# Modulation weights in tiles of 2048 columns, four blocks of 512 to the array together

## The chip, the cores and the metric

The kernel runs on one core of a Trainium2 chip. The metric is the device time of one execution in microseconds (us), and the time of a version is the median of its runs. TensorE (PE) does the matrix products, VectorE (DVE), ScalarE (ACT) and GpSimd (POOL) the elementwise work. SyncE's queue (SP) issues nearly all transfers between the device's memory and the on-chip memory, in order: an issue that waits holds up those behind it. A product's result lies in PSUM, a small accumulation memory of banks of 512 columns by 128 partitions. All data is f32.

## The reference, cut to what matters

The model has two layers on 1024 latent tokens and 256 context tokens of width 1024. Each layer begins with a modulation: two vectors (`c` for the latents, `c_ctx` for the context) pass through silu and are multiplied by a matrix of 1024 x 6144; the six slices of the result shift, scale and gate what follows.

```
s_lat = silu(c); s_ctx = silu(c_ctx)
for layer in range(2):
    sh1, sc1, g1, sh2, sc2, g2 = split(s_lat @ ada_w[layer] + ada_b[layer], 6)
    csh1, ..., cg2             = split(s_ctx @ ada_w[layer] + ada_b[layer], 6)
    h = modulate(rmsnorm(x, norm_mix_w[layer]), sh1, sc1)      # the context likewise
    x = x + g1 * mixer(h)                                      # layer 0: attention + SSD, layer 1: mLSTM
    x = x + g2 * mlp(modulate(rmsnorm(x, ...), sh2, sc2))
out = rmsnorm(x, final_norm_w)
```

Each mixer begins with an input projection, a product of `h` with a matrix of some 2100 or 3100 columns, parts of which go through a convolution of five taps along the tokens.

## The kernel before, in words

**The modulation.** Its weight, 2 x 24 MB, is far larger than the two vectors that it multiplies, so the vectors are the stationary operand and the weight streams through the array. `ada_group` (L182) computes a group, 2048 of the 6144 columns of one layer (three groups to a layer). It walks the 1024 input rows in eight steps `k` of 128. In a step the 2048 columns are four blocks of 512. The stationary operand has only 32 columns, so each block uses a strip of 32 columns of the array and writes its own 32 partitions of one PSUM bank: block g goes to partitions 32g to 32g+31. The argument `per` is the number of blocks that one weight tile holds. With `per=4` a step is one load of 128 x 2048 (1 MB) and four products; with `per=2` it is two loads of 128 x 1024 (512 KB), each with two products. In the trace each product appears as two instructions, so a tile of two blocks is a row of `x4` and one of four blocks is `x8`. After a step the generator yields. After the eighth, DVE copies the bank (`ada_rows`), PE turns it with eight small instructions (`ada_t`), and DVE adds the bias into `mods`. The bank is the only one of its kind (`bufs=1`), so a group begins when the one before has been turned.

**Where the groups run.** The first group (layer 0, group 0) is computed in `start` (L433) with `per=4` and eight buffers, beside the load of `x`. Three more (`(0,1)`, `(0,2)`, `(1,0)`) run as a filler inside `in_proj0` (L487), the other two (`(1,1)`, `(1,2)`) as a filler inside `in_proj1` (L1283), all with `per=2`, from a pool of two and of three buffers. The method `fill(n)` advances the filler by n steps, and is called each time a block of a projection has been evacuated.

**The projections.** `lin` (L383) multiplies a weight tile of 128 columns with the three token blocks (512, 512 and 256 tokens). Weight and data are each split into a high and a low part, and three products (`mm3`, L99 to L101) make one f32 product: 24 instructions for a block. In `in_proj0` eight such weight tiles feed the convolution (`conv_silu`, L401, five DVE operations of 1284 elements). Then come four tiles for the low-rank inputs of the attention (`lc`, `lsq`, `lhi`, `llo`: pool `s0a`) and four for the gate `z`. When the convolution is through, the filler is replaced by `back_states` (L731), the backward chain of the state-space scan, from the pool `bwd`. `in_proj1` has eight tiles for its convolution and then the values.

**Pools.** Pools are laid out as a stack in the on-chip memory. A pool opened where a closed one was waits, tile by tile, for the last reader of the old tile. `ada1` stands below the pool of the convolution and stays open to the end of `in_proj0`; `ada2` stands below `s1`, `raw1` and `kN`.

**The order of the work.** The order of instructions on each engine is fixed when the kernel is built: a planner takes them by priority (the order of the program, or further ahead where `high_priority` says so; `ahead`, L84, gives each filler step in `in_proj1` a lead of 400) and by its own estimate of when their operands are ready. On the chip each engine then runs its list in order. The four lines that step the modulation:

```
nc.sync.dma_start(out=raw, in_=w[k * 128:(k + 1) * 128, c0:c0 + per * 512])
for g in range(per):
    nc.tensor.matmul(out=ps[32 * (n + g):32 * (n + g) + 32, :], lhsT=self.s32[:, 2 * k:2 * k + 32],
                     rhs=raw[:, g * 512:(g + 1) * 512], start=k == 0, stop=k == KT - 1)
```

Of the kernel before, what the change touches and what calls it, by code (L numbers as in the profile page):

```python
# [67 lines left out]
class Kernel:  # L68
# [418 lines left out]
    def in_proj0(self):  # L487
# [23 lines left out]
        wp, pp = self.wp0, self.pp0  # L511
        with ExitStack() as es:
# [1 line left out]
            xp = self.pool("xnbn", side="right", stack=es)  # L514
            xn = xp.tile([128, NC, 512], F32, name="xn")
            bn = xp.tile([128, NC, 256], F32, name="bn")
            ap = self.pool("ada1", bufs=2, stack=es)
            stp = self.pool("ps_l0", bufs=2, space=PSUM, stack=es)
            self.filler = self.ada_fill(ap, stp, ((0, 1), (0, 2), (1, 0)), 2)


            with ExitStack() as es2:
# [27 lines left out]
            with ExitStack() as es2:  # L550
# [14 lines left out]
                for m in range(8):  # L565
# [17 lines left out]
                    if m < 6:  # L583
                        last = (m, co)
            self.fill(99)
            nc.sync.dma_start(out=self.xnd, in_=xn)
            nc.sync.dma_start(out=self.bnd, in_=bn)
            bp = self.pool("bwd", bufs=2, stack=es)
# [694 lines left out]
    def in_proj1(self):  # L1283
        nc, I = self.nc, self.ins
        w_in = I["od_w_in"][0]
        dram = self.dram.tile
        self.od = dram([128, 8, SEQ], F32, name="od")
        self.vd = dram([128, NC, D], F32, name="vd")
        self.kTd = dram([128, 4, NT], F32, name="kTd")
        self.qTd = dram([128, 4, SEQ], F32, name="qTd")  # L1290
        self.kNd = dram([128, NC, 512], F32, name="kNd")
        self.o1 = ExitStack()
        op = self.pool("out1", side="right", stack=self.o1)
        self.uN, self.wt, self.em = (op.tile([128, 160], F32, name=n) for n in ("uN", "wt", "em"))
        self.keepc = op.tile([128, 2, NC, 4], F32, name="keepc")
        gb = op.tile([128, 32], F32, name="gbias")
        for i, n in enumerate(("od_i_bias", "od_f_bias")):
            nc.sync.dma_start(out=gb[:, 16 * i:16 * i + 16],
                              in_=I[n].rearrange("e d h -> (e d h)").unsqueeze(0).to_broadcast([128, 16]))
        every, lat = [(b, ALL_BLOCKS[b]) for b in (0, 2, 1)], list(enumerate(LAT_BLOCKS))  # L1300
        self.in1, self.banks = ExitStack(), ExitStack()
        p1 = self.pool("ps_m1", space=PSUM, stack=self.in1)
        p2 = self.pool("ps_m2", space=PSUM, stack=self.banks)
        self.pp = pp = Banks(m1=(p1, "m1", 2), m2=(p2, "m2", 3), st=(p2, "st", 2), ada=(p2, "ada", 1), mm=(p2, "m2", 3),
                             a=(p2, "m2", 3))
        self.wp1 = wp = self.pool("w1", bufs=2, stack=self.in1)
        vps = ExitStack()
        vp = self.pool("wv1", bufs=2, side="right", stack=vps)
        with ExitStack() as es2:
            ap = self.pool("ada2", bufs=3, stack=es2)  # L1310
            self.filler = self.ahead(self.ada_fill(ap, pp, ((1, 1), (1, 2)), 2), 400)
            sp = self.pool("s1", bufs=2, stack=es2)
            with self.tc.high_priority(400):
                raws = self.conv_raw(self.pool("raw1", stack=es2), 2)
            kNp = self.pool("kN", bufs=2, stack=es2)

            def by_token(m, co):
                kN = kNp.tile([128, NC, 128], F32, name="kN")
                for c0 in range(0, NC, 4):
                    n = min(4, NC - c0)  # L1320
                    o = c0 * 128 + (4 if c0 >= 8 else 0)
                    ps = pp.tile([128, 512], F32, name="kN_ps", tag="a")
                    for i in range(n):
                        self.turn(ps[:, i * 128:(i + 1) * 128], co[:, o + i * 128:o + (i + 1) * 128])
                    nc.scalar.copy(out=kN[:, c0:c0 + n, :], in_=ps[:, :n * 128].rearrange("p (c f) -> p c f", f=128))
                nc.sync.dma_start(out=self.kNd[:, :, m * 128:(m + 1) * 128], in_=kN)

            last = None
            self.fill(4)
            for m in (4, 5, 6, 7, 0, 1, 2, 3):  # L1330
                whi, wlo = self.w4 if m == 4 else self.load_w(wp, w_in[:, m * 128:(m + 1) * 128])
                r = raws[m % 2]

                def evac(b, t0, nb, ps):
                    o = t0 + 2 if t0 < SEQ else t0 + 6
                    with self.tc.high_priority(400 if m == 4 else 0):
                        nc.scalar.copy(out=r[:, o:o + nb], in_=ps[:, :nb])
                    self.fill(2 if b == 0 else 1)

                self.lin(pp, whi, wlo, 128, self.h, every if m >= 4 else lat, evac, tag="m1")  # L1340
                if last is not None:
                    by_token(*last)
                    last = None
                co = self.conv_silu(sp, r, m, 1, None, m >= 4)
                if m >= 4:
                    last = (m - 4, co)
                    nc.sync.dma_start(out=self.kTd[:, m - 4, 0:SEQ], in_=co[:, 0:SEQ])
                    nc.sync.dma_start(out=self.kTd[:, m - 4, SEQ:NT], in_=co[:, SEQ + 4:NT + 4])
                else:
                    nc.sync.dma_start(out=self.qTd[:, m, :], in_=co[:, 0:SEQ])  # L1350
            self.fill(99)


        with ExitStack() as es2:
            tp = self.pool("ml_g", stack=es2)
            self.gN = tp.tile([128, NC, 32], F32, name="gN")
            for j in range(4):
                n = 256 if j else 288
                hi = vp.tile([128, KT, 288], F32R, name="wv_hi")
                lo = vp.tile([128, KT, 288], F32R, name="wv_lo")  # L1360
                for i in range(2 if j else 3):
                    raw = wp.tile([128, KT, 128], F32, name="w_raw", tag="w_raw")
                    c0, M = (1024 + j * 256 + i * 128, 128) if i < 2 else (3072, 32)
                    nc.sync.dma_start(out=raw[:, :, :M], in_=w_in[:, c0:c0 + M].rearrange("(k p) f -> p k f", p=128))
                    self.split_w(raw[:, :, :M], hi[:, :, i * 128:i * 128 + M], lo[:, :, i * 128:i * 128 + M])
                for c in range(NC):
                    b = min(c // 4, 2)
                    o = c * 128 - ALL_BLOCKS[b][0]
                    ps = pp.tile([128, 512], F32, name="v1_ps", tag="m1")
                    for k in range(KT):  # L1370
                        xh, xl = (self.h[b][i][:, k, o:o + 128] for i in range(2))
                        self.mm3(ps[:, :n], xh, xl, hi[:, k, :n], lo[:, k, :n], k == 0, k == KT - 1)
                    st = vp.tile([128, 256], F32, name="v_stg", tag="v_stg", bufs=2)
                    nc.vector.tensor_copy(out=st, in_=ps[:, :256])
                    nc.sync.dma_start(out=self.vd[:, c, j * 256:(j + 1) * 256], in_=st)
                    if j == 0:
                        nc.vector.tensor_tensor(out=self.gN[:, c, :], in0=ps[:, 256:288], in1=gb, op=ALU.add)
                    self.fill(1)
                if j == 0:
                    self.filler = self.gates(tp, pp)  # L1380
            self.fill(99)
        vps.close()
        self.banks.close()
# [1035 lines left out]
```

## Time and profile before

| | |
|---|---|
| median of 3 runs | 3176.93 us (3168.58 to 3180.64) |
| the profiled execution | 3181.18 us |
| its span in the profile | 3179.4 us |
| TensorE busy | 2938.7 us, 92% |
| VectorE, ScalarE, GpSimd busy | 1905.1, 1370.1, 978.7 us |
| TensorE's granted clock over the span | 0.969 of 2.4 GHz |

The span runs from the first instruction to the last; 1.8 us of the execution lie around it. A wait is put down to what ended last before the waiting instruction could start. "xN" in a row is the number of instructions merged into it. PE is the product itself, PEld the load of its stationary operand, which overlaps it. Products overlap at their ends, so the time that one takes from the next is read from start to start, and not from the duration.

### The profile page before, as it was taken

Reading aid. Unit: us, or ns where it says so; the run is one execution under the profiler, and the core shown is the slowest. Engines: PE = TensorE matmul, PEld = TensorE weight load, DVE = VectorE, ACT = ScalarE, POOL = GpSimd, SP = SyncE. Lnnn points to the kernel's source line nnn. Section 1 sums busy time; section 2 is a strip of 40 time slices with the busy share of each in tenths; the row PEclk is TensorE's granted clock in tenths of the full one; section 3 lists DMA queues with packets and bytes.
Section 4 is the critical chain, followed back from the end, with each engine's and each line's share of the span. In section 5 each row is a group of like instructions: output and inputs, shape, how many; then the busy total and the mean of one; then the engine's idle time right before and its main releaser. Section 6 shows DMA issues by size and latency. Waiting matters only on the chain. (4 is left out here: it accounts for less than half of the span.)

```text
span 3179.4 us, 43747 instructions
## 1 busy us (share of the span) xinstructions
PE 2938.7 (92%) x16097; PEld 2408.2 (76%) x16097; DVE 1905.1 (60%) x3393; ACT 1370.1 (43%) x2424; POOL 978.7 (31%) x754
## 2 busy tenths in 40 slices
PE   6999889999998999989999969999788888989998
PEld 3666778878886888878888836897676777868887
DVE  5444148878747664437667854522577765457777
ACT  5322267777625554443223332112443644543333
POOL 2113245563113443222121221215343443322223
PEclk8999989999999999999999979999999999999999
DMA  7565474443442453364333256239683355465432
GB/s 268 172 215 181 154 272 125 128 129 93 154 157 99 152 184 122 123 242 159 104 115 116 82 158 191 88 101 269 191 220 114 110 176 182 155 235 168 151 125 77
DMA packets 336986, 497.47 MB, mean 156 GB/s; under 512 B 29668, under 2 KB 199876, under 8 KB 335108
## 3 DMA queue, kind: packets, MB, share of 16 engines
q1 hardware_dynamic: 316132, 460.58, 45.3%
q10 hardware_dynamic: 20640, 34.09, 2.9%
q8 instruction: 127, 2.08, 0.3%
q14 instruction: 87, 0.71, 0.1%
HBM read 345.43 MB, written 149.16 MB: 156 GB/s over the span
## 5 line engine op out<-in xcount | busy, mean ns | idle before, releaser
L1783 POOL TENSOR_TENSOR wu<-S,wu 128x512 fp32r<-128x512 f32 (+1 forms) x117 | 211.8, 1812 | 580.4 <-ACT wu L1782 527.5
L1783 POOL TENSOR_TENSOR wu<-w_raw,wu 128x512 fp32r<-128x512 f32 (+1 forms) x106 | 175.4, 1658 | 318.4 <-ACT wu L1782 296.5
L1782 ACT CAST wu<-S 128x512 fp32r<-128x512 f32 (+1 forms) x192 | 141.7, 746 | 302.9 <-PE z_ps L101 64.0
L99 PE MATMUL lin_ps<-hhi,w_hi 128*128 128x512 f32 (+3 forms) x696 | 263.8, 379 | 5.9 <-ACT hhi L363 2.9
L100 PE MATMUL lin_ps<-hlo,w_hi 128*128 128x512 f32 (+3 forms) x696 | 261.2, 375 | 2.2 <-DVE hlo L364 1.2
L101 PE MATMUL lin_ps<-hhi,w_lo 128*128 128x512 f32 (+3 forms) x696 | 260.4, 374 | 0.0
L1782 ACT CAST wu<-w_raw 128x512 fp32r<-128x512 f32 (+1 forms) x186 | 135.5, 737 | 211.7 <-PE y_ps L101 101.3
L99 PE MATMUL y_ps<-hh,wu 128*128 128x512 f32 x480 | 188.8, 393 | 18.0 <-ACT wu L1782 13.3
L110 POOL TENSOR_TENSOR w_lo<-w_raw,w_hi 128x1024 fp32r<-128x1024 f32 (+1 forms) x33 | 78.6, 2384 | 361.1 <-ACT w_hi L109 299.6
L99 PE MATMUL y_ps<-hu,wu 128*128 128x512 f32 x448 | 177.8, 397 | 12.7 <-DVE c L1879 8.3
L100 PE MATMUL y_ps<-hh,wu 128*128 128x512 f32 x480 | 188.0, 392 | 0.0
L101 PE MATMUL y_ps<-hh,wu 128*128 128x512 f32 x480 | 186.1, 390 | 0.0
L100 PE MATMUL y_ps<-hu,wu 128*128 128x512 f32 x448 | 176.9, 395 | 0.9 <-DVE hu L1783 0.9
L101 PE MATMUL y_ps<-hu,wu 128*128 128x512 f32 x448 | 176.1, 394 | 0.0
L99 PEld LDWEIGHTS lin_ps<-hhi,w_hi 128*128 128x128 f32 (+1 forms) x696 | 132.1, 190 | 51.4 <-issue 19.1
L100 PEld LDWEIGHTS lin_ps<-hlo,w_hi 128*128 128x128 f32 (+1 forms) x696 | 132.0, 190 | 44.2 <-issue 20.1
L101 PEld LDWEIGHTS lin_ps<-hhi,w_lo 128*128 128x128 f32 (+1 forms) x696 | 132.0, 190 | 36.9 <-issue 16.9
L1783 DVE TENSOR_TENSOR hh<-h_raw,hh 128x1024 fp32r<-128x1024 f32 (+1 forms) x110 | 141.3, 1295 | 20.1 <-ACT hh L1782 20.1
L1782 ACT CAST hh<-h_raw 128x1024 fp32r<-128x1024 f32 x114 | 109.0, 994 | 89.6 <-DMA h_raw<-hd 48.8
L100 PE MATMUL r_ps<-hh,wu 128*128 128x512 f32 x360 | 141.2, 392 | 4.1 <-DVE hh L1783 4.1
L99 PE MATMUL r_ps<-hh,wu 128*128 128x512 f32 x360 | 140.8, 392 | 3.7 <-ACT hh L1782 2.6
L99 PE MATMUL x_ps<-hc,wu 128*128 128x256 f32 x496 | 139.5, 283 | 3.3 <-ACT hc L1982 3.3
(429 smaller groups left out, 8626.5 us busy)
## 6 DMA issues: line engine op xcount, KB each, us to landing
h_raw<-hd SPq DMA_DIRECT2D x96, 512.0 KB, 3.6
ada_raw<-in_ada_w_dram SPq DMA_DIRECT2D x80, 512.0 KB, 4.3
w_raw<-in_mlp_w_dram SPq DMA_DIRECT2D x72, 512.0 KB, 3.9
hd<-c SPq DMA_DIRECT2D x120, 256.0 KB, 3.6
w_raw<-in_mlp_w_dram SPq DMA_DIRECT2D x28, 1024.0 KB, 8.0
hd<-c ACTq DMA_DIRECT2D x90, 256.0 KB, 2.3
x<-xd SPq DMA_DIRECT2D x32, 512.0 KB, 7.6
xd<-x SPq DMA_DIRECT2D x24, 512.0 KB, 3.2
```

Of the source, the lines that this page charges most:

```text
L99: mm(out=out, lhsT=whi, rhs=xhi, start=first, stop=False)
L100: mm(out=out, lhsT=whi, rhs=xlo, start=False, stop=False)
L101: mm(out=out, lhsT=wlo, rhs=xhi, start=False, stop=last)
L110: self.nc.gpsimd.tensor_tensor(out=lo, in0=raw, in1=hi, op=ALU.subtract)
L1782: self.nc.scalar.copy(out=to[:, 0], in_=src)
L1783: eng.tensor_tensor(out=to[:, 1], in0=src, in1=to[:, 0], op=ALU.subtract)
```

## The change

The fillers' weight tiles hold four blocks (`per` has its default 4) instead of two. `ada1` keeps two buffers, which are now 8 KB to a partition instead of 4; `ada2` goes from three buffers of 4 KB to two of 8. `ada1` gets a stack of its own, `ea`, and is closed when the convolution part of `in_proj0` has been issued, so that `bwd` and the pools behind it lie where `ada1` was.

```
-            ap = self.pool("ada1", bufs=2, stack=es)
+            ea = ExitStack()
+            ap = self.pool("ada1", bufs=2, stack=ea)
             stp = self.pool("ps_l0", bufs=2, space=PSUM, stack=es)
-            self.filler = self.ada_fill(ap, stp, ((0, 1), (0, 2), (1, 0)), 2)
+            self.filler = self.ada_fill(ap, stp, ((0, 1), (0, 2), (1, 0)))
...
             self.fill(99)
+            ea.close()
             nc.sync.dma_start(out=self.xnd, in_=xn)
...
-            ap = self.pool("ada2", bufs=3, stack=es2)
-            self.filler = self.ahead(self.ada_fill(ap, pp, ((1, 1), (1, 2)), 2), 400)
+            ap = self.pool("ada2", bufs=2, stack=es2)
+            self.filler = self.ahead(self.ada_fill(ap, pp, ((1, 1), (1, 2))), 400)
```

## Rows read from the trace of the kernel before

**Rows 1.** The page: busy time of each engine, share of the span, instructions.
```profile
PE 2938.7 (92%) x16097; PEld 2408.2 (76%) x16097; DVE 1905.1 (60%) x3393; ACT 1370.1 (43%) x2424; POOL 978.7 (31%) x754
```

**Rows 2.** Windows: stretch and length, busy PE, PEld, DVE, ACT, POOL, clock, DMA, GB/s.
```profile
80.00:310.00 230.00, 230.00 (x1147) 155.35 (x1146) 106.52 (x122) 62.25 (x97) 41.00 (x29) 1.00 0.59 190
310.00:388.00 78.00, 77.43 (x411) 63.38 (x410) 19.30 (x60) 21.68 (x49) 20.95 (x16) 1.00 0.43 144
1850.00:1880.00 30.00, 18.78 (x77) 9.37 (x77) 13.81 (x24) 14.82 (x28) 11.06 (x10) 0.70 0.31 98
1880.00:2000.00 120.00, 120.00 (x567) 79.98 (x564) 54.55 (x42) 31.63 (x46) 20.83 (x9) 1.00 0.61 187
```

**Rows 3.** Waits of PE, 1840 to 2000: total, times, longest.
```profile
PE ada_ps L194 <- DMA ada_raw<-in_ada_w_dram: 11.2, 1, 11.2
```

**Rows 4.** Timeline of PE around a two-block tile: start, us, engine, line, instruction, count.
```profile
218.41 0.40 PE L101 MATMUL lin_ps<-hhi,w_lo 128*128 128x512 f32 x1
218.73 1.05 PE L194 MATMUL ada_ps<-ada_raw,s 128*32 128x512 f32 x4
219.72 0.50 PE L99 MATMUL lin_ps<-hhi,w_hi 128*128 128x512 f32 x1
220.05 0.39 PE L100 MATMUL lin_ps<-hlo,w_hi 128*128 128x512 f32 x1
220.28 0.40 PE L101 MATMUL lin_ps<-hhi,w_lo 128*128 128x512 f32 x1
```

**Rows 5.** Timeline of PE where two such tiles stand side by side.
```profile
159.40 0.39 PE L100 MATMUL lin_ps<-hlo,w_hi 128*128 128x512 f32 x1
159.71 1.06 PE L194 MATMUL ada_ps<-ada_raw,s 128*32 128x512 f32 x8
160.71 0.50 PE L101 MATMUL lin_ps<-hhi,w_lo 128*128 128x512 f32 x1
```

**Rows 6.** Windows of the instructions on ada_ps: stretch, PE, PEld, DVE, clock, DMA.
```profile
80.00:310.00 230.00, 48.42 (x192) 6.65 (x192) 2.07 (x3) 1.00 0.59 190
1850.00:1970.00 120.00, 34.17 (x128) 4.79 (x128) 1.39 (x2) 0.93 0.57 179
```

**Rows 7.** Timeline of PE, the modulation's rows of in_proj1 that aren't single full-clock tiles.
```profile
1850.22 3.62 PE L194 MATMUL ada_ps<-ada_raw,s 128*32 128x512 f32 x12
...
1870.07 1.92 PE L194 MATMUL ada_ps<-ada_raw,s 128*32 128x512 f32 x4 [11.22 <-DMA ada_raw<-in_ada_w_dram]
...
1873.92 1.46 PE L194 MATMUL ada_ps<-ada_raw,s 128*32 128x512 f32 x4
...
1918.98 1.91 PE L194 MATMUL ada_ps<-ada_raw,s 128*32 128x512 f32 x12
```

**Rows 8.** Timeline of PE, the first four-block tile in start, clock at half.
```profile
16.55 1.94 PE L194 MATMUL ada_ps<-ada_raw,s 128*32 128x512 f32 x8
```

**Rows 9.** SP queue: a wait (1820 to 1970), and the issues behind it.
```profile
SPq L1298 <- DVE nt L367: 19.4, 1, 19.4
...
1865.87 15.33 SPq L192 DMA_DIRECT2D ada_raw<-in_ada_w_dram  x7
```

**Rows 10.** DMA issues: 80 to 310, whole span, 0 to 45: count, KB, us to landing.
```profile
ada_raw<-in_ada_w_dram SPq DMA_DIRECT2D x48, 512.0 KB, 4.1
...
w_raw<-in_mlp_w_dram SPq DMA_DIRECT2D x28, 1024.0 KB, 8.0
...
xin<-in_x_dram SPq DMA_DIRECT2D x8, 512.0 KB, 10.6
```

**Rows 11.** Timeline: ACT's first `lc`, after the convolution; PE's last `ada_t` of in_proj0.
```profile
254.89 0.59 ACT L602 COPY lc<-lin_ps 128x512 f32<-128x512 f32 x1 [5.01 <-DMA xbcd<-conv_acc]
...
304.87 0.96 PE L204 MATMUL ada_t<-ident,ada_rows 128*128 128x8 f32 x8
```

**Rows 12.** Timeline after in_proj0: SP's last stores, then PE's first wait.
```profile
372.68 14.10 SPq L630 DMA_DIRECT2D zd<-stg  x4
...
395.27 0.80 PE L797 MATMUL cb_ps<-xT_c 128*128 128x128 f32 x2 [6.66 <-DMA xT_c<-xbcd]
```

## The prediction

> **What bounds the kernel now.** I read the page first: TensorE is busy for 92% of the span, no other engine for more than 60% [rows 1]. A share of the whole says little about two stretches, so the windows came next, cut where the modulation's fillers run. In stage A (`in_proj0`, 80 to 310 us) PE is busy for 230.00 of 230 us at granted clock 1.00, the upper of its two levels, 2.4 GHz. DVE is busy for 106.5 us, ACT for 62, POOL for 41, the DMA engines for 59%. From 1880 to 2000, most of stage B (`in_proj1`), PE is busy for 120.00 of 120 us, again at 1.00. Between 1850 and 1880 it is not: 18.8 of 30 us, clock 0.70 [rows 2]. The waits name the hole: once, for 11.2 us, PE waits for a modulation weight [rows 3]. The reader should see that where the fillers run, every PE instruction that goes away shortens the stretch, but for one place where a transfer decides.
>
> **What a tile costs.** Here the timeline decides, start to start. Projection products of 512 columns follow each other every 0.23 us (220.05 to 220.28). Around a two-block tile they start at 218.41 and 220.05, 1.64 us, with one tile and two product steps between: the tile takes 1.64 - 2 x 0.23 = 1.18 us, 0.99 of it its own and 0.19 at its edges [rows 4]. Twice in stage A two tiles of one step happened to be issued side by side. That is what the changed kernel does by construction, and it took 1.00 us from 159.71 to 160.71, with the same edge ahead of it (159.40 to 159.71); edges counted alike, 1.19 us [rows 5]. So four blocks cost what two cost, since each block has its own 32 columns of the array.
>
> Here the Trainium skill speaks against the change (TensorE: Matmul & The Clock Gate, Part 3: Packing small matmuls, under "Measured speedup vs the span model"): four tiles packed by rows gave 3.07 times the speed of one, not four. If a four-block tile lost as much against a two-block one, an estimate from that figure makes it 0.99 x 4/3.07 = 1.29 us, and the change would give 40 x 0.30 = 12 us less than below, inside the forecast's own range. The row on this very tile says 1.00 against 0.99, and the row decides.
>
> **Stage A.** 192 instructions on `ada_ps` [rows 6] are 44 two-block tiles and two side-by-side pairs: 44 x 1.18 + 2 x 1.19 = 54.3 us. Afterwards three groups of eight steps are 24 four-block tiles: 24 x 1.19 = 28.6 us. Saved: 25.7 us.
>
> **Stage B.** 128 instructions [rows 6]. Four entries are not single tiles at full clock: 3.62 us for three tiles at the start, 1.92 and 1.46 us for the two after the hole, all with the clock below full, and 1.91 us for three tiles in a row [rows 7]. That last one shows the limit of the packing: eight instructions took 1.00 us [rows 5], twelve 1.91, since the third tile uses strips that are taken. The remaining 96 instructions are 24 single tiles, 28.3 us. With 0.1 us for the edge of the 1.91 entry this is 3.6 + 1.9 + 1.5 + 2.0 + 28.3 = 37.3 us. Afterwards: 16 tiles, of which I leave three at half clock, at 1.94 us each, the price of the first four-block tile of the kernel [rows 8], and 13 at 1.19: 5.8 + 15.5 = 21.3 us. Saved: 16.0 us.
>
> **The hole at 1858.** The fourth load of stage B sits on SP behind an issue (L1298) that waits 19.4 us for the norm's buffers. It leaves at 1865.87 [rows 9] and lands as PE's wait ends, at 1870.07: 4.2 us [rows 7]. The change leaves L1298 where it is. Two whole steps will now be loaded ahead of it instead of one and a half, and the third step's load still leaves at 1865.9. Best case: the planner puts that tile so late that PE works through the hole, worth up to 10 us (the wait less what the norm would hold back anyway). Worst: 1 MB takes 8.0 us to land as the MLP's loads do [rows 10], 4 us more than now. I take 0, nearest to the row: the load that decides leaves at the same time.
>
> **The loads.** Each byte is loaded once, before and after. SP issues 40 loads instead of 80, after as many waits for a tile to be read, so its other issues stand behind fewer of them. In stage A a 512 KB load lands after 4.1 us [rows 10], and PE never waits for one there. Two 4 KB buffers are one step of lead, two 8 KB buffers are two. By the rows 1 MB lands after 4.1 us (as a half does now) to 10.6 us (the loads of `x`, behind each other in a full queue) [rows 10]; with 24 steps in the 160 us up to the last convolution block (ACT's first `lc` is at 254.89 [rows 11]), 6.7 us a step, a buffer has 2 x 6.7 - 1.2 = 12 us from one read to the next. I take 0; the other end is a rival below. The DMA engines' 59% [rows 2] hold the same bytes in 204 us at 66%.
>
> **The pools.** `ada1` is closed early, and `lc`, `bwd` and `stg` move onto it: ACT's first `lc` copy, at 254.89 after 5.0 us for a store of the convolution, will wait instead for the last group's `ada_t`. That now comes at 304.87 [rows 11], as the fillers lag far behind the convolution. If it still did, ACT would stand 50 us, and PE would stop after three PSUM banks (0.23 x 24 x 2 + 0.12 x 24 = 14 us of products). With two steps of lead I expect the groups to keep up with `fill`, which offers 24 steps within the convolution, so that the last `ada_t` comes within those 14 us: cost 0. The other end: 20 us, if the fillers end 34 us after the convolution (a group's eight steps at 4.2 us a load).
>
> **What is late next.** Stage A's time is passed on: PE is busy for 77.4 of the next 78 us [rows 2], then waits 6.7 us for loads that SP issues behind the last `zd` stores [rows 12], which follow the last projection and move with it. Stage B runs on into products that keep PE full to 2000.
>
> **Sum.** 25.7 + 16.0 = 41.7 us. The profiled execution took 3181.2 us, so it would take 3139.5; it lies 4.3 us above the median of its runs, 3176.9, against which the forecast is **3135 us**, 1.3% less. About 0.5%, 16 us, is what a measurement can tell from no change.
>
> **Rivals.**
> 1. *Given back in part.* The pool wait costs 20 us and the hole 4 us: 3135 + 24 = 3159. For it: the lag of 50 us in rows 11. Against it: that lag comes from a lead of one step, which doubles. Chance 0.16.
> 2. *A stage bound by its loads.* If the loads can't be drawn faster than the 190 GB/s of stage A [rows 2], PE's time there becomes waiting: only stage B's 16 us are left, 3161; if B's 187 GB/s [rows 2] is a limit too, nothing, 3177. Against it: PE waits for no load there now, so the rate is what PE asks for. The same 3177 comes out if the planner puts projection products between the four blocks so that they don't run together; against that, every two-block tile stands whole. Chance 0.12.
> 3. *Slower: 1 MB lands too late at every step.* PE's list is fixed, and a tile that has not landed stops all that stands behind it. The change saves 41.7/40 = 1.04 us a step. A wait of 1.04 us at each step takes all of it; 1.44 us makes the kernel slower by 16 us; 2.5 us, about a quarter of the one such wait in rows 3, gives 3135 + 100 = 3235 in all 40 steps, and 3195 in the 24 of stage A. It decides if a load takes more than those 12 us. For it: that wait exists, and 10.6 us in a full queue comes near. Against it: 8.0 us for the other loads of this size. Chance 0.09.
>
> **How the numbers follow.** The forecast has 0.63: 3135 us, its own range 3117 to 3150 (the hole gone, -10, and 8 us for the spread of the runs, which was 12 us before; up: 12 us for the smaller back-payments). The range of all: 3113 to 3168, which takes in rival 1 and the first case of rival 2. Faster by over 0.5% (under 3161): the forecast, rival 1 and a little of rival 2, 0.80. Within 0.5%: most of rival 2, 0.11. Slower: rival 3, 0.09.
>
> **What would show it.** Right: all of the fillers' `ada_ps` entries are `x8` at 1.0 us to the next start; PE stays busy for 100% of both stages, A ending 20 to 30 us sooner, the rest shifted whole; the last `ada_t` of `in_proj0` before about 245 us. Wrong: waits of PE on `ada_raw` of more than 12 us in all, an idle PE at the first `lc` copies with ACT waiting on `ada_t`, or four-block tiles longer than 1.2 us at full clock.

## The result, and the profile after

The changed kernel takes 3128.3 us (median of 4 runs, 3124.1 to 3131.6) against 3178.8 us for the kernel before on the same chip: the ratio is 0.9848, 95% interval 0.983 to 0.9866, 50 us less. (The 3176.9 us that the forecast started from is the median of three of the four runs before that are counted here.) The forecast was 3135 us and 42 us less. The profiled execution took 3125.6 us. That is 55.6 us less than the profiled one of before: the one lies 2.8 us below its median, the other 2.4 above the 3178.8.

The page's first row, the counterpart of [rows 1]: PE loses 52 us of busy time, and its share stays 92%.

```profile
PE 2887.0 (92%) x16097; PEld 2395.2 (77%) x16097; DVE 1896.3 (61%) x3393; ACT 1372.7 (44%) x2424; POOL 974.6 (31%) x754
```

The windows, cut at the new ends of the fillers (columns as in [rows 2]): stage A (to 235), the rest of `in_proj0` (to 363), the start of stage B, and stage B.

```profile
80.00:235.00 155.00, 155.00 (x887) 112.04 (x887) 79.36 (x74) 48.53 (x73) 26.09 (x17) 1.00 0.72 249
235.00:363.00 128.00, 127.02 (x669) 104.17 (x668) 39.53 (x108) 37.12 (x76) 41.23 (x31) 1.00 0.46 156
1812.00:1833.00 21.00, 10.33 (x46) 5.93 (x44) 13.53 (x23) 13.44 (x25) 10.19 (x15) 0.74 0.19 63
1833.00:1951.00 118.00, 117.77 (x624) 87.91 (x625) 60.31 (x46) 32.90 (x47) 27.01 (x12) 0.98 0.63 208
```

PE is as full as before, in stage A at clock 1.00, in stage B at 0.98 (1.00 before). It waits for no weight of the modulation in stage A. The loads now run at 249 GB/s in stage A, where [rows 2] had 190, and a load of 1 MB lands after 5.0 us (median, 80 to 310):

```profile
ada_raw<-in_ada_w_dram SPq DMA_DIRECT2D x24, 1024.0 KB, 5.0
```

The tile itself, against [rows 4] and [rows 5], and the sum of the tiles, against [rows 6]:

```profile
101.77 0.39 PE L101 MATMUL lin_ps<-hhi,w_lo 128*128 128x512 f32 x1
102.09 1.07 PE L194 MATMUL ada_ps<-ada_raw,s 128*32 128x512 f32 x8
103.08 0.50 PE L99 MATMUL lin_ps<-hhi,w_hi 128*128 128x512 f32 x1
103.42 0.39 PE L100 MATMUL lin_ps<-hlo,w_hi 128*128 128x512 f32 x1
```
```profile
80.00:310.00 230.00, 25.57 (x192) 3.78 (x192) 2.06 (x3) 1.00 0.60 206
1800.00:1970.00 170.00, 19.22 (x128) 2.96 (x128) 1.39 (x2) 0.92 0.52 170
```

Four blocks take 0.99 us from start to start and 1.65 - 0.46 = 1.19 with their edges, as read from the pair of before. As many instructions as before (192 and 128) fill 25.6 and 19.2 us instead of 48.4 and 34.2. The hole at the start of stage B is still there: the load that PE waits for leaves SP behind the two loads of the gate bias (`gbias`), as in [rows 9]. The last group of stage A is turned at 233 instead of 305 us [rows 11], 8 us ahead of ACT's first `lc` copy:

```profile
PE ada_ps L194 <- DMA ada_raw<-in_ada_w_dram: 10.9, 1, 10.9
```
```profile
1826.90 0.34 SPq L1300 DMA_DIRECT2D gbias<-in_od_i_bias_dram  x1
...
1827.77 21.68 SPq L192 DMA_DIRECT2D ada_raw<-in_ada_w_dram  x6
```
```profile
233.36 0.95 PE L204 MATMUL ada_t<-ident,ada_rows 128*128 128x8 f32 x8
...
241.31 0.59 ACT L604 COPY lc<-lin_ps 128x512 f32<-128x512 f32 x1
```

Where the 50 us come from is best seen by landmarks, first or last starts of instructions in the profiled executions: ACT's last `stg` (end of `in_proj0`), PE's first product of the queries (`up_ps<-cq`), DVE's first normalised token block of layer 1 (`nt<-x`), PE's first product of the values (`v_ps`). Lengths in us:

| stretch | before | after | gain |
|---|---|---|---|
| start to end of `in_proj0` | 388.7 | 363.7 | 25.0 |
| from there to the first queries | 51.6 | 36.6 | 15.0 |
| to the first normalised block of layer 1 | 1391.2 | 1393.4 | -2.2 |
| to the first values (stage B) | 174.1 | 156.8 | 17.3 |
| to the end of the span | 1173.8 | 1173.4 | 0.4 |

The first and the fourth row are what was forecast: 25.7 and 16.0. The second, 15 us where no instruction was changed, was not. There SP's queue tells the story: before, the weights of the attention's first projection (`wa_raw` from `ev_w_ukv`) and their input (`ckv`) were issued behind the last stores of the gate `z`:

```profile
389.11 0.32 SPq L630 DMA_DIRECT2D zd<-stg  x1
...
391.72 0.81 SPq L944 DMA_DIRECT2D wa_raw<-in_ev_w_ukv_dram  x2
392.57 4.50 SPq L918 DMA_DIRECT2D ckv<-ckvd  x6
```

After the change (line numbers two higher) they are issued 17 us ahead of the last such store, among the stores of earlier blocks:

```profile
346.58 1.02 SPq L946 DMA_DIRECT2D wa_raw<-in_ev_w_ukv_dram  x2
347.69 0.38 SPq L632 DMA_DIRECT2D zd<-stg  x1
348.12 3.46 SPq L920 DMA_DIRECT2D ckv<-ckvd  x4
...
364.08 0.32 SPq L632 DMA_DIRECT2D zd<-stg  x1
...
364.96 0.53 SPq L758 DMA_DIRECT2D xT_c<-xbcd  x1
```

Before, PE had stood still from 388.6 to 395.3 for `xT_c`, the input of the scan [rows 12], and for 4.1 us more, to 400.2, for `ckv`; it then worked at a granted clock that had fallen towards the lower of its levels. The load of `xT_c` is behind the last `zd` store after the change too, as the last line shows. But with `wa_raw` and `ckv` there, PE begins on their products at once and comes to `xT_c` only when it has landed:

```profile
363.42 0.39 PE L99 MATMUL up_ps<-ckv,wa_hi 128*128 128x512 f32 x1
...
370.37 0.39 PE L799 MATMUL cb_ps<-xT_c 128*128 128x128 f32 x2
```

In windows of before, PE is busy for 1.41 of 12 us, then for 12.40 of 15, both at 0.73. After, the same 27 us begin with 12 full ones at 1.00:

```profile
388.00:400.00 12.00, 1.41 (x8) 0.91 (x6) 0.00 (x0) 7.28 (x13) 3.92 (x5) 0.73 0.83 282
400.00:415.00 15.00, 12.40 (x43) 9.69 (x44) 3.62 (x6) 9.28 (x16) 8.38 (x10) 0.73 0.64 215
```
```profile
363.00:375.00 12.00, 12.00 (x64) 10.23 (x64) 2.99 (x6) 10.09 (x18) 4.79 (x5) 1.00 0.83 268
375.00:390.00 15.00, 10.27 (x59) 8.98 (x57) 4.71 (x9) 8.85 (x17) 5.43 (x6) 0.89 0.93 313
```

Over the whole stretch, before and after:

```profile
388.70:440.30 51.60, 35.02 (x194) 30.32 (x195) 13.15 (x29) 25.09 (x52) 15.03 (x16) 0.83 0.89 302
363.70:400.30 36.60, 31.31 (x195) 28.21 (x194) 13.24 (x29) 23.75 (x48) 11.27 (x12) 0.95 0.95 326
```

PE's idle time fell from 16.6 to 5.3 us, and about the same number of products took 3.7 us less at the higher clock. Together that is the 15 us.

Why the loads can go earlier is in the addresses of the built programs. Pool `att_wkv` holds `wa_raw` at 140.4 to 148.4 KB of each partition, in both. Before, the three `stg` buffers lay at 142.8 to 148.8 KB, nearly all of them inside it, so that the load had to wait for the last of them to be stored. With `ada1` closed early they lie at 132.8 to 138.8 KB.

### The profile page after: what moved, and what is told of

It is laid out like the page before. It is cut to its first block, busy times and chain, and to the rows that moved or that the text cites. A ratio compares the mean times of both kernels' runs of the same rounds, so it can differ in the third digit from the quotient of the medians.

```text
span 3123.9 us, 43712 instructions
## 1 busy us (share of the span) xinstructions
PE 2887.0 (92%) x16097; PEld 2395.2 (77%) x16097; DVE 1896.3 (61%) x3393; ACT 1372.7 (44%) x2424; POOL 974.6 (31%) x754
## 5 line engine op out<-in xcount | busy, mean ns | idle before, releaser
L99 PEld LDWEIGHTS lin_ps<-hhi,w_hi 128*128 128x128 f32 (+1 forms) x696 | 132.4, 190 | 45.8 <-issue 15.9
```

Of the source, the lines that this page charges most:

```text
L99: mm(out=out, lhsT=whi, rhs=xhi, start=first, stop=False)
```

## The experiments

Two theories were to be told apart. *Three separate gains*: the packing in A, the layout behind A, the packing in B. Its rivals: the 15 us come from fillers that end earlier, not from the layout; and the gain of A and B comes from half as many loads and interruptions, or from the longer lead of the loads, not from four blocks side by side. Times are medians with the ratio to the kernel before, run on the same chip; the stretches are those of the table above.

| kernel | us | ratio, 95% | `in_proj0` ends | to queries | stage B |
|---|---|---|---|---|---|
| before | 3178 to 3180 | | 388.7 | 51.6 | 174.1 |
| after | 3128.3 | 0.983 to 0.9866 | 363.7 | 36.6 | 156.8 |
| e1, A alone | 3145.7 | 0.9877 to 0.9908 | 364.9 | 36.7 | 174.0 |
| e2, B alone | 3169.7 | 0.9959 to 0.9982 | 389.3 | 52.3 | 157.0 |
| e3, old addresses | 3144.2 | 0.9873 to 0.9903 | 361.3 | 51.4 | 157.1 |
| e4, two strips | 3167.0 | 0.9946 to 0.9971 | 384.6 | 36.2 | 169.1 |
| e5, closing alone | 3166.3 | 0.9948 to 0.9974 | 387.2 | 37.6 | 174.0 |
| e6, half tiles, four buffers | 3135.0 | 0.9838 to 0.9879 | 365.0 | 36.8 | 156.6 |
| e7, bias among constants | 3123.0 | 0.9802 to 0.9844 | 364.8 | 36.4 | 145.9 |
| e8, one buffer | 3126.4 | 0.9825 to 0.9867 | 365.8 | 35.2 | 156.9 |
| e9, after again | 3129.2 | 0.9835 to 0.9863 | 364.7 | 36.6 | 156.9 |
| e10, e7 again | 3116.0 | 0.9795 to 0.9824 | 364.3 | 37.0 | 146.2 |

**Stage A alone (e1) and stage B alone (e2).** The changed lines of the other stage are put back.

> Stage A as in the changed kernel (four-block tiles, ada1 closed early), stage B as before (two-block tiles, three buffers). Theory: the 50 us are three separate gains: about 25 us in stage A from the packing, about 14 us just behind it (the attention's first weights load earlier, since the closing of ada1 moved the z stage's buffers out from under them), 17 us in stage B, and a few us lost again later. So this kernel keeps the first two: the last z evacuation near 364 us, the first queries' product near 400 us, 3178.8 - 36 = 3143 us. Rival, that the 14 us hang on the fillers' faster loads as a whole and on stage B too: nothing of it is missing here only if stage B's tiles matter, then 3155 or more.

> Stage B as in the changed kernel, stage A and ada1 as before. Theory of three separate gains: 17 us less than before, 3162 us, with the 11 us hole of PE in stage B still there and the first queries' product still near 440 us. Rival, that the stages are not independent: a time that does not make up, with the kernel that has stage A alone, the 50 us of both.

e1 came out at 3145.7: stage A and the stretch behind it as in the changed kernel, stage B as before. e2 has its 17 us in stage B and nothing elsewhere, but its median is only 9.4 us below the kernel before (6 to 13 by the interval), not 17. PE's list up to stage B is the same as before there, and yet the stretch up to the normalised block took 3.9 us more and the stretch behind the values 5.7 us more in its profile. Its profile is also that of the slowest of its six runs, 5.6 us above the median. Such differences need not be the change's: the second of these stretches took 1173.4 and 1176.8 us in two executions of the changed kernel, and 1177.9 and 1171.0 in two of the kernel of e7. But the spread may not be all: in the three profiles of kernels whose stage B is that of before, this last stretch took 1170.8 to 1173.8 us, in the nine with the changed stage B 1170.9 to 1180.4. A part of stage B's gain may be given back there; no run tells. The two gains, 33.4 and 9.4, make up 43 of the 50 us; whether the rest is this spread is open. The stretches themselves add up.

**The old addresses (e3).** An unused pool of 10 KB pushes `bwd`, `stg` and `s0a` back to where they lay.

```
+            pad = self.pool("pad", stack=es).tile([128, 2560], F32, name="pad")
             bp = self.pool("bwd", bufs=2, stack=es)
```

> The changed kernel with an unused pool of 10 KB a partition opened just before bwd, so that bwd, the z stage's buffers and the low-rank pool lie at the addresses that they had before the change; the tiles, the loads and the closing of ada1 stay as changed. Layout theory: the first attention weights (wa_raw, ckv) again overlap the z stage's last buffers, are again issued only behind the last zd store, PE is again idle for about 10 us at the start of the attention with its clock at half behind that, and 12 to 15 us of the gain go: 3140 to 3143 us. Rival (the 14 us come from fillers that end earlier, so that SP and the other engines are freer in the z stage): no change, 3128 us.

3144.2 us, and the stretch to the queries is 51.4 us again. SP issues the loads behind the last `zd` store, and PE waits as it did in [rows 12]:

```profile
361.66 0.32 SPq L633 DMA_DIRECT2D zd<-stg  x1
364.37 0.81 SPq L947 DMA_DIRECT2D wa_raw<-in_ev_w_ukv_dram  x2
365.22 4.67 SPq L921 DMA_DIRECT2D ckv<-ckvd  x6
```
```profile
368.20 0.80 PE L800 MATMUL cb_ps<-xT_c 128*128 128x128 f32 x2 [7.04 <-DMA xT_c<-xbcd]
373.24 0.76 PE L99 MATMUL up_ps<-ckv,wa_hi 128*128 128x512 f32 x1 [4.24 <-DMA ckv<-ckvd]
```

The fillers ended early here too (the last group is turned at 231), so the rival falls: the 15 us are the layout's. (`in_proj0` itself ends 2.4 us sooner in this kernel than in the changed one, so that the first queries come 12.4 us later, while the medians differ by 15.9.)

**Two strips (e4).** All of the change, but the blocks share two strips of the array instead of four (and DVE copies the lower half of the bank twice, in two instructions):

```
-                    nc.tensor.matmul(out=ps[32 * (n + g):32 * (n + g) + 32, :], ..., start=k == 0, stop=k == KT - 1)
+                    nc.tensor.matmul(out=ps[32 * (g % 2):32 * (g % 2) + 32, :], ...,
+                                     start=k == 0 and g < 2, stop=k == KT - 1 and g > 1)
```

> The changed kernel in which blocks 2 and 3 of a tile go to the strips of blocks 0 and 1, on whose sums they are added, so that only two blocks of a step can run side by side (the modulation is wrong by that; loads, buffers, pools and the number of products are as changed). Packing theory: a tile takes two passes of the array, 1.84 us to the next start as the twelve instructions in a row did before, instead of 1.00: 40 tiles x 0.84 = 34 us on the path, up to 7 us more in the first group: 3162 to 3169 us. Rival (the gain comes from fewer loads, waits and interruptions, 40 instead of 80): 3128 us, or up to 8 us more.

3167.0 us. A tile takes 1.84 us to the next start, nearly twice the 0.99 of two blocks:

```profile
105.13 1.91 PE L194 MATMUL ada_ps<-ada_raw,s 128*32 128x512 f32 x8
106.97 0.50 PE L99 MATMUL lin_ps<-hhi,w_hi 128*128 128x512 f32 x1
```

Against the changed kernel stage A is 20.9 us longer (24 x 0.85 = 20.4) and stage B 12.3 (16 x 0.85 = 13.6). This kernel still has half as many loads and interruptions as the kernel before, and against that one its stage A ends 4.1 us sooner and its stage B is 5.0 us shorter: that is the most that the rival can claim of the 25.0 and 17.3. The halved edges alone would make 24 x 0.19 = 4.6 and 16 x 0.19 = 3.0 us. Of the 38.7 us between the medians of this and the changed kernel the two stages have 33.2. In the profile the stretch up to layer 1 was 6.8 us longer as well (1400.2 us), and no run says why.

**The closing alone (e5).** The kernel before, with only the stack `ea` and its early closing.

> The kernel before with the early closing of ada1 alone: two-block tiles and buffers as before in both stages. Layout theory: the attention's first weights no longer overlap the z stage's buffers, so that the queries begin 12 to 15 us earlier, and nothing else changes: 3165 us. Rival (the early closing has a price when the fillers lag: the backward chain's pool now lies where the modulation tiles were, which are read until 305 us, and its nine steps come 50 us later, into the z stage or past it): 3179 us or more.

3166.3 us: the layout's gain without any packing, 13.6 us, with 37.6 us to the queries. The price that the rival named is real in its mechanism and does not show in the time. The backward chain (`st_ps`), which began at 256 us before, now waits for the modulation's last tiles:

```profile
L723 PE MATMUL st_ps<-xe,bn x36: 377/379/483, 307.2 to 332.7; 128*128 128x256 f32 x36
```

It still ends at 333, when the attention's first products (386.95) are 54 us off.

**Half tiles with four buffers (e6).** In stage A, `per=2` again, with `bufs=4`.

> The changed kernel, but in stage A with two-block tiles of 512 KB in four buffers: the same memory, the same addresses, the same lead of two steps, and stage B as changed. Theory (what counts is that four blocks are issued side by side, and one tile forces that): the two halves of a step land apart and are issued apart in most steps, each such step costs 1.18 us more, 24 at most: 3128 + up to 28, 3145 to 3156 us, and the excess is the number of separate tiles in stage A times 1.18 us. Rival (the lead of two steps is what counts): the halves meet, and the time is that of the changed kernel, 3128 us.

My theory was wrong here and the rival nearly right. With the lead of two steps the planner put the two halves of a step side by side in 21 of 24 steps, unasked. The other three look like this:

```profile
191.04 1.05 PE L194 MATMUL ada_ps<-ada_raw,s 128*32 128x512 f32 x4
193.63 1.05 PE L194 MATMUL ada_ps<-ada_raw,s 128*32 128x512 f32 x4
```

Stage A ends 1.3 us later than in the changed kernel, where three more tiles would make 3.5. The times, 3135.0 against 3128.3, can't be told apart by their intervals.

**One buffer (e8).** `bufs=1` for `ada1`, tiles of four blocks.

> The changed kernel with one buffer of 1 MB instead of two in stage A: four blocks to a tile, but the lead of one step that the kernel before had, in the same memory as then. It tells the width of the tile from the lead, after half tiles with the lead of two steps gave nearly all of the gain. Theory (either one brings the four blocks together; the width does it without the lead): all 24 tiles of stage A are issued whole at 1.00 us, the fillers end some 50 us later than in the changed kernel, nothing waits for them but the backward chain, which has room: 3128 to 3133 us. Rival (the lead is needed as well): PE waits for landings in stage A, or the low-rank copies wait for the last group: 3145 us or more.

3126.4 us, the same as the changed kernel. The tiles are whole and the sum is 25.96 us; the last group is turned at 308, as late as before:

```profile
80.00:310.00 230.00, 25.96 (x192) 4.00 (x192) 2.06 (x3) 1.00 0.58 194
```
```profile
308.47 0.96 PE L204 MATMUL ada_t<-ident,ada_rows 128*128 128x8 f32 x8
```

So either the width or the lead brings the blocks together, and neither is needed beside the other. The late fillers cost nothing here. But this is no test of the wait that the prediction feared for the low-rank copies: by the addresses, `ada1` with one buffer ends at 134.8 KB and `lc` begins at 138.8, so that only `bwd` and `stg` lie on it. In the changed kernel `ada1` reaches to 142.8 KB, and `lc`'s first tile lies on it.

**The bias among the constants (e7, e10).** The hole of stage B was untouched, so its cause was taken away: the gate bias gets memory that no other tile used.

```
-        gb = op.tile([128, 32], F32, name="gbias")
+        gb = self.const.tile([128, 32], F32, name="gbias")
```

> The changed kernel with the gate bias of in_proj1 in the pool of constants, 128 bytes a partition that were never used by another tile, so that its two loads no longer wait on SP for the norm's buffers and the third modulation load of stage B isn't held up behind them. Theory: the wait of PE of 10.9 us at the start of stage B goes, and 6 to 10 us of the time with it: 3118 to 3122 us. Rival (PE would wait for the normalised tokens there anyway): PE's wait changes its name, and the time stays within 3 us of 3128.

3123.0 us (ratio 0.9802 to 0.9844), a microsecond above the range expected. The bias is now loaded at 44.5 us, and the load that PE waited for leaves SP 13.6 us sooner than in the changed kernel:

```profile
1814.19 30.71 SPq L192 DMA_DIRECT2D ada_raw<-in_ada_w_dram  x7
```

The wait on `ada_raw` is gone from PE's list between 1790 and 1980; in its place stand 1.7 us for an evacuation:

```profile
PE rs_bc L106 <- DVE rst L246: 15.6, 1, 15.6
PE rs_nat L300 <- DVE sqa L289: 5.4, 1, 5.4
PE lin_ps L99 <- ACT conv_raw L1339: 1.7, 1, 1.7
```

Stage B takes 145.9 us, 10.9 less. (The constants grow by 128 bytes and push most other tiles up by as much, so that not every small difference elsewhere need be the hole's.) To see how much of it lasts, the changed kernel and this one ran once more on one chip.

> The changed kernel once more, on the same chip as the others of this call, for the comparison: 3128 us within 4 us.

> The kernel with the gate bias among the constants once more, beside the changed kernel on the same chip: 5 to 8 us below it, since its stage B was 10.6 us shorter in the profile and some 4 us of that were lost again later.

e9 gave 3129.2 us (ratio 0.9835 to 0.9863), e10 3116.0 (0.9795 to 0.9824): 13 us below the changed kernel, more than was expected, and the intervals do not meet. Stage B has 10.7 of them. The last stretch, 1176.8 against 1171.0 us in these two profiles, has 5.8, and in the earlier two profiles it went the other way (1173.4 and 1177.9); so the hole is worth some 11 us, and what goes beyond is no more than this stretch varies by itself. This is the fastest version of the study, 1.9% below the kernel before.

## Why the prediction was right, and where it was not

*What bounds the kernel.* Right: PE was the bound of both stages, and what was taken from it came off the time. The landmarks give 25.0 and 17.3 us, the sum of tiles had 25.7 and 16.0.

*What a tile costs.* Right: 0.99 us to the next start, where [rows 5] had 1.00; e4 shows that the gain goes when the strips are shared. The loss of 0.30 us a tile that was estimated from the Trainium skill (TensorE: Matmul & The Clock Gate, Part 3: Packing small matmuls) did not appear: 0.99 us for four blocks against 0.99 for two. That figure is for tiles packed by rows; these blocks lie side by side in columns.

*The hole at 1858.* Right in cause and size: 10.9 us against 11.2, behind the same issue of SP; e7 takes the issue out of the way and the hole goes. The best case in the text, up to 10 us, was about what the hole was worth (10.9 in e7), though by another way than the planner's.

*The loads.* Cost 0, as taken. Rivals 2 and 3 fall with it: stage A drew 249 GB/s, PE waited for no modulation load there, and 1 MB landed after 5.0 us, near the lower end of the 4.1 to 10.6 that the text allowed.

*The pools.* The cost, 0, was right, and for the reason given: with two steps of lead the last `ada_t` (233) comes ahead of the first `lc` copy (241). What a lag would have cost is not shown; in e5 and e8, where the fillers lag to 305 and 308, `lc` does not lie on `ada1`. What the step missed is its other side. It went through what would lie on `ada1`'s old place, and not what the moved pools would set free: the 10 KB by which `stg` slid from under the attention's first weights. Those 15 us are missing from the sum. The forecast fell short by 13.9 us between the profiled executions (55.6 against 41.7), and by 8.8 between the medians (50.5).

*What is late next.* This is the step that failed. It said that the wait of 6.7 us behind the last `zd` stores [rows 12] moves with the projection. Instead it went, though the load of `xT_c` is still issued behind those stores: the loads of `wa_raw` and `ckv` left before them, so that PE had other products to do, idled for 5.3 us of the stretch instead of 16.6, and kept a clock of 0.95 instead of 0.83. [rows 12] do not show the two loads that decided; the next issues on SP's queue would have. An issue that stands behind the last store of a stage can be a sign of memory that this stage holds, as with `wa_raw`. It need not be, as `xT_c` shows, and only the addresses tell.

*The range.* That 3128.3 us lies in the forecast's own range of 3117 to 3150 owes something to luck: below 3135 it had room for the hole and for the spread of the runs, and the term that came was another.

## What to carry to other kernels

Price a repeated item by the gap from its start to its neighbour's, and look for places where the present kernel happens to do what the change does always: two such places gave this forecast its main term to within a microsecond (25.7 us against 25.0). When a change closes, grows or moves a pool, list what lies above it at both addresses, and for every load of the next stage which old tile it waits for; here 10 KB of layout were worth 13.6 us (e5) to 15.9 (e3), over a quarter of the gain, and 128 bytes of bias in fresh memory some 11 us more. Where a load comes late off an in-order queue, look at the issues ahead of it: one of them may be the one that waits.

## What the runs showed of the hardware

Products of 32 stationary columns on the four strips of the array ran side by side at no cost that the trace can show: 0.99 us for one pair and for two. On shared strips they took 1.84. Going from full-width products to strips and back cost 0.19 us, around two blocks as around four (0.20 around the four on shared strips). The granted clock was 0.73 in the 27 us around a PE idle of some 11 us at the start of the attention, and 1.00, then 0.89, where that idle was gone; so the 15 us there are 11.3 of waiting and 3.7 of slower products.
